# A fused low-rank update on one core: the order of the first loads and stores, and setup work moved between engines

## The chip, the core and the metric

The kernel runs on one core of a Trainium2 chip. The core has a matrix engine (TensorE, PE in the profile), a vector engine (VectorE, DVE), a scalar engine (ScalarE, ACT), a general engine (GpSimd, POOL) and SyncE (SP), which here only issues transfers. Each engine has its own instruction stream; they meet through semaphores. Sixteen DMA engines move data between the chip's memory (HBM) and the on-chip memory (SBUF). The metric is the device time of one execution in microseconds, the median over runs.

## The reference

```python
batch, seq, d_model, r = 16, 512, 768, 16
# x: (16, 512, 768) float32, A: (768, 16), B: (16, 768), scale: 0.5

def reference(x, A, B, scale):
    lora = np.matmul(np.matmul(x, A), B)
    return (x + scale * lora).astype(np.float32)
```

So 25.17 MB are read, a rank-16 product is added to them, and 25.17 MB are written. A and B are 48 KB each.

## The kernel before

**Tiles and parts.** The 8192 rows of `x` are 64 tiles of 128 rows x 768. They are loaded in seven parts, `PARTS = [2, 6, 8, 16, 16, 14, 2]` tiles, one DMA each. Within a part, each of the 128 partitions holds neighbouring rows of memory, so a part of 2 tiles moves in pieces of 6 KB, one of 6 in 18 KB, of 8 in 24 KB, of 16 in 48 KB. All of `x` but the last part has room in SBUF (`x_all`, 62 tiles); the last two tiles go where tiles 0 and 1 were, once these are stored. The 14 tiles of part 5 land last of the others, and until then their room (`spare`) is lent to the setup: `a_rows`, `a_t`, `w_one`, `b_rows`, `b_half`, `pick`.

**Setup.** GpSimd zeroes `a_rows` (L175), `b_rows` (L176), `pick`, `w_bd` and `y_bd`, and makes `pick` a selection pattern. A (L139) and B (L143) are loaded into every eighth row. VectorE transposes A (L214) and makes `w_one` with three small casts (L221); ScalarE copies `w_one` to the four diagonal blocks of `w_bd` (L201). ScalarE casts B to fp16 (`b_half`, L195), TensorE spreads it by `pick` (L290), and ScalarE copies the result to `b_mm` (L198).

**Groups.** The tiles are worked on in eight groups of 8, each in two halves of 4 (`h` = 0, 1):

1. `narrowed` (L171): a half is cast to fp16 in `xh[h]`, half 0 by ScalarE, half 1 by GpSimd. It waits for the loads of its tiles and, by `s_y`, for the matmuls that read the half before.
2. `turned` (L230): VectorE transposes the half in 32x32 blocks.
3. `projected` (L260): TensorE multiplies by `w_bd` in 24 matmuls and leaves x A in `ps_yt`; `s_y` counts the halves.
4. ScalarE (L209) scales that into the diagonal blocks of `y_bd`, four small instructions for a group.
5. `raised` (L277): TensorE multiplies by `b_mm` into `lora_ps`, two tiles at a time, in one of two buffers.
6. `summed` (L235): VectorE adds that to `x_all`, two tiles at a time.

TensorE runs this as a loop of eight passes: the first pass raises an empty group ahead of the first projection, and each pass raises the group before. VectorE's order is written out by hand: the transpose of a half of the next group, then the adds of two pairs of this one. So an engine that waits in its own order holds up all that stands behind it there.

**Transfers.** All of them are issued by SP, in this order: loads of parts 0 and 1, A (once its room is zeroed), B (once its room is zeroed), loads of parts 2, 3 and 4; then, after the first projection (`s_y`), the load of part 5 into the lent room; then the stores of `STORES`, each of which waits on `s_sum` until the groups that it holds are added (a count of groups + 2, raised by TensorE in `raised(1)` of the pass after the one that raises the group), or on `s_last` for the last group. After the store of part 1, SP waits for the store of part 0 to land (`s_out0`) and issues the load of part 6. One queue takes all of it in order.

**The end.** GpSimd waits for the last add, clears most of the semaphores, waits for the stores, and clears the others.

Of the kernel before, what the change touches and what calls it, by code (L numbers as in the profile page):

```python
# [13 lines left out]
PARTS = [2, 6, 8, 16, 16, 14, 2]  # L14
# [6 lines left out]
APART = 8  # L21
# [3 lines left out]
def kernel(  # L25
# [8 lines left out]
    nc = tc.nc  # L34
    fp32 = mybir.dt.float32
    P = 128
    Q = 32
    NQ = P // Q
# [4 lines left out]
    R = A.shape[1]  # L43
    NC = D // 64
# [6 lines left out]
    def sb(name, shape, dtype):  # L51
        return nc.alloc_sbuf_tensor(name, shape, dtype).ap()
# [11 lines left out]
    def lent(n):  # L64
        taken[0] += n
        return spare[:, ds(taken[0] - n, n)]
# [6 lines left out]
    a_t = lent(2 * R * Q).rearrange("p (k r c) -> p k r c", k=2, r=R)  # L73
    w_one = lent(NC * R)[0:Q].bitcast(MM_DT).rearrange("p (c k r) -> p c k r", c=NC, k=2)
    b_rows = lent(D)
    b_half = lent(D // 2).bitcast(MM_DT)
    pick = lent(P // 2).bitcast(MM_DT).rearrange("p (b r) -> p b r", b=NQ)
    w_bd = sb("w_bd", [P, NC, 2, P], MM_DT)
    b_mm = sb("b_mm", [P, D], MM_DT)
    xh = [sb(f"xh{h}", [P, SUB, D], MM_DT) for h in range(2)]  # L80
    y_bd = sb("y_bd", [P, GROUP, P], MM_DT)
    lora = [ps(f"lora_ps{i}", [P, 2, D]) for i in range(2)]
    y_ps = ps("ps_yt", [P, GROUP, Q])

    sems = []

    def sem(name):
        sems.append(nc.alloc_semaphore(name))
        return sems[-1]


    parts = []
# [7 lines left out]
    def memory(t2, i, s, n):  # L100
        S = PARTS[i]
        return t2[ds(parts[i], S * P), :].rearrange("(p s) d -> p s d", s=S)[:, ds(s, n), :]

    def held(i, s, n):
        return tiles(where.index((i, s)), n)

    def tiles(t, n):
        return x_all[:, ds(t % ROOM, n), :]

    s_load = [sem(f"s_load{i}") for i in range(len(PARTS))]  # L110
    s_a, s_b = sem("s_a"), sem("s_b")
    s_ready, s_brows, s_pick, s_zero = sem("s_ready"), sem("s_brows"), sem("s_pick"), sem("s_zero")
    s_w, s_bh, s_bp, s_bm = sem("s_w"), sem("s_bh"), sem("s_bp"), sem("s_bm")
    s_narrow = [sem(f"s_narrow{h}") for h in range(2)]
    s_y, s_spread = sem("s_y"), sem("s_spread")
    s_turned = [sem(f"s_turned{h}") for h in range(2)]
    s_lora = sem("s_lora")

    s_free = [sem(f"s_free{p}") for p in range(PAIRS)]

    s_sum, s_last, s_out0, s_out = sem("s_sum"), sem("s_last"), sem("s_out0"), sem("s_out")

    MMS = 2 * NC
    STORES = [
        (0, 0, 2), (1, 0, 6), (2, 0, 8), (3, 0, 16), (4, 0, 16), (5, 0, 8), (5, 8, 6), (6, 0, 2)
    ]

    section = ExitStack()
# [2 lines left out]
    def on_sync(e):  # L131
        def load(i):
            ld = (i, 0, PARTS[i])
            e.dma_start(out=held(*ld), in_=memory(x2, *ld)).then_inc(s_load[i], 16)

        load(0)
        load(1)
        e.wait_ge(s_ready, 1)
        e.dma_start(  # L139
            out=a_rows[0 : NC * APART : APART, :], in_=A.rearrange("(c e) r -> c (e r)", e=64)  # L140
        ).then_inc(s_a, 16)
        e.wait_ge(s_brows, 1)
        e.dma_start(out=b_rows[0 : R * APART : APART, :], in_=B).then_inc(s_b, 16)  # L143
        for i in range(2, len(PARTS) - 2):
            load(i)

        e.wait_ge(s_y, 1)
        load(len(PARTS) - 2)
        for st in STORES:
            i, s, n = st  # L150
            groups = where.index((i, s + n - 1)) // GROUP + 1
            if groups < NG:

                e.wait_ge(s_sum, groups + 2)
            else:
                e.wait_ge(s_last, 1)
            ins = e.dma_start(out=memory(out2, *st), in_=held(*st))
            ins.then_inc(s_out if i else s_out0, 16)
            if i == 1:
                e.wait_ge(s_out0, 16)  # L160
                load(len(PARTS) - 1)

    def narrowed(e, copy, g, h):
        t = g * GROUP + h * SUB
        for i in dict.fromkeys(where[t + k][0] for k in range(SUB)):
            e.wait_ge(s_load[i], 16)
        if g:
            e.wait_ge(s_y, 2 * g + h - 1)
        n = SUB if (t + SUB - 1) // ROOM == t // ROOM else SUB // 2
        for k in range(0, SUB, n):  # L170
            last = copy(out=xh[h][:, ds(k, n), :], in_=tiles(t + k, n))  # L171
        last.then_inc(s_narrow[h], 1)

    def on_gpsimd(e):
        e.memset(a_rows[0 : NC * APART], 0.0).then_inc(s_ready, 1)  # L175
        e.memset(b_rows, 0.0).then_inc(s_brows, 1)  # L176

        e.sem_inc(s_spread, 1)
        for p, s in enumerate(s_free):
            e.sem_inc(s, 1 if p < 2 else 2)  # L180
        e.memset(pick, 0.0).then_inc(s_pick, 1)
        e.memset(w_bd.rearrange("p c k m -> p (c k m)").bitcast(fp32), 0.0)  # L182
        e.memset(y_bd.rearrange("p s m -> p (s m)").bitcast(fp32), 0.0)  # L183
        e.wait_ge(s_pick, 1)
        e.affine_select(  # L185
            out=pick, in_=pick, compare_op=mybir.AluOpType.not_equal, fill=1.0, base=0,
            pattern=[[0, NQ], [-APART, Q]], channel_multiplier=1,
        ).then_inc(s_zero, 1)
        for g in range(NG):
            narrowed(e, e.tensor_copy, g, 1)  # L190

    def on_scalar(e):
        e.wait_ge(s_zero, 1)
        e.wait_ge(s_b, 16)
        e.copy(out=b_half, in_=b_rows).then_inc(s_bh, 1)  # L195
        narrowed(e, e.copy, 0, 0)
        e.wait_ge(s_bp, 1)
        e.copy(out=b_mm, in_=lora[0][:, 0, :]).then_inc(s_bm, 1)  # L198
        e.wait_ge(s_ready, 3)
        for b in range(NQ):  # L200
            last = e.copy(out=w_bd[ds(b * Q, Q), :, :, ds(b * Q, R)], in_=w_one)  # L201
        last.then_inc(s_w, 1)
        for g in range(NG):
            if g + 1 < NG:
                narrowed(e, e.copy, g + 1, 0)
            e.wait_ge(s_y, 2 * g + 2)
            for b in range(NQ):
                q = ds(b * Q, Q)
                last = e.mul(out=y_bd[q, :, q], in_=y_ps[q, :, :], mul=sc)  # L209
            last.then_inc(s_spread, 1)  # L210

    def on_vector(e):
        e.wait_ge(s_a, 16)
        e.transpose(  # L214
            out=a_t[0 : NC * APART].rearrange("i k r c -> i (k r) c"),
            in_=a_rows[0 : NC * APART].rearrange("c (i k r) -> c (k r) i", k=2, r=R),
        ).then_inc(s_ready, 1)
        e.wait_ge(s_ready, 2)
        EACH = Q // APART
        for b in range(NC // EACH):  # L220
            last = e.tensor_copy(  # L221
                out=w_one[:, ds(b * EACH, EACH), :, :],
                in_=a_t[ds(b * Q, Q)].rearrange("i k r (c n) -> i c k r n", n=APART)[..., 0],
            )
        last.then_inc(s_ready, 1)

        def turned(g, h):
            e.wait_ge(s_narrow[h], g + 1)
            v = xh[h].bitcast(fp32)
            e.transpose(out=v, in_=v).then_inc(s_turned[h], 1)  # L230

        def summed(g, p):
            xs = tiles(g * GROUP + 2 * p, 2)
            e.wait_ge(s_lora, (g + 1) * PAIRS + p + 1)
            ins = e.tensor_tensor(out=xs, in0=xs, in1=lora[p % 2], op=mybir.AluOpType.add)  # L235
            if g + 1 < NG or p + 2 < PAIRS:
                ins.then_inc(s_free[p], 1)
            elif p + 1 == PAIRS:
                ins.then_inc(s_last, 1)

        turned(0, 0)

        e.wait_ge(s_lora, 1)
        turned(0, 1)
        for g in range(NG):
            for h in range(2):
                if g + 1 < NG:
                    turned(g + 1, h)
                summed(g, 2 * h)
                summed(g, 2 * h + 1)  # L250

    def on_tensor(e):
# [15 lines left out]
        def raised(p):  # L268
# [16 lines left out]
                mms[2].then_inc(s_sum, 1)  # L285
            mms[-1].then_inc(s_lora, 1)

        e.wait_ge(s_bh, 1)
        for n0, w in ((0, 512), (512, 256)):
            last = e.matmul(  # L290
                lora[0][:, 0, ds(n0, w)], pick.rearrange("p b r -> p (b r)"),
                b_half[:, ds(n0, w)], start=True, stop=True,
            )
        last.then_inc(s_bp, 1)
        e.wait_ge(s_bm, 1)
        e.wait_ge(s_w, 1)
        with e.Fori(0, NG):
            for h in range(2):
                raised(2 * h)
# [2 lines left out]
        for p in range(PAIRS):  # L302
            raised(p)

    on_sync(nc.sync)
    on_gpsimd(nc.gpsimd)
    on_scalar(nc.scalar)
    on_vector(nc.vector)
    on_tensor(nc.tensor)

    nums = [s.num for s in sems]
    assert nums == list(range(nums[0], nums[0] + len(nums)))

    nc.gpsimd.wait_ge(s_last, 1)
    nc.gpsimd.sem_clear(range(nums[0], s_sum.num))
    nc.gpsimd.wait_ge(s_out, (len(STORES) - 1) * 16)
    nc.gpsimd.sem_clear(range(s_sum.num, s_out.num + 1))
    section.close()


# [33 lines left out]
```

## Time and profile before

| what | value |
|---|---|
| median of 3 runs | 125.58 us (125.11 to 126.81) |
| the profiled execution | 124.85 us |
| its span, first to last instruction | 122.7 us |
| HBM read, written | 25.26 MB, 25.17 MB, 411 GB/s over the span |
| DMA queue | 2216 packets, 96.8% of 16 engines' span |
| PE, PEld, DVE, ACT, POOL busy | 46%, 30%, 68%, 32%, 21% |
| adds (L235), 32 | 54.1 us, 1733 ns each |
| transposes (L230), 16 | 28.2 us, 1765 ns each |
| casts (L171) on POOL, ACT | 22.1 us, 22.0 us; 2.75 us for half a group |
| mean granted TensorE clock | 0.901 |

The span is what the profile shows of the program; the device time holds some 2 us more around it. Busy shares are of the span. "PEclk" is the clock granted to TensorE in tenths of full speed, "PEld" its weight loads. In the tables by stretch each engine has its busy us and number of instructions, then come the clock, the share of the DMA engines in use, and GB/s, where a packet counts in the stretch in which it starts. A row of SP ("SPq") is the issue of a transfer, not the transfer. "issue" in the chain is time in which an engine waited for nothing that the profile shows.

### The profile page before, as it was taken

The numbers are of one execution on the slowest core, as the hardware profiler recorded it, in microseconds if no ns is written. First come the engines' busy times: TensorE is split into PE (matmuls) and PEld (weight loads), VectorE is DVE, ScalarE is ACT, GpSimd is POOL, SyncE is SP. The second block draws the span as 40 slices with busy tenths as digits, with TensorE's granted clock in tenths as the row PEclk, the third lists the DMA queues.
The fourth block names the chain that finished last, engine by engine and source line by source line (L and its number), as shares of the span: only waits on it lengthen the run. The fifth ranks groups of instructions, "written<-read, shape, count | busy, mean of one in ns | idle before, by whom it ended". The sixth has DMA issues, their size and how long they took to land.

```text
span 122.7 us, 1317 instructions
## 1 busy us (share of the span) xinstructions
PE 56.3 (46%) x530; PEld 37.1 (30%) x530; DVE 83.9 (68%) x52; ACT 38.7 (32%) x47; POOL 26.2 (21%) x19
## 2 busy tenths in 40 slices
PE   0000206976755764844845775576497545000000
PEld 0000003855343452533614534345354422000000
DVE  0003751418999999999999999999979979600000
ACT  0002992092193534254084072353400310000000
POOL 7503500026017008006204401700530000000000
PEclk9999999999999999999999999998559999655555
DMA  3999998899799699999599999899796996898994
GB/s 88 439 433 403 449 529 385 385 513 465 305 513 481 288 513 449 449 435 435 202 449 413 479 401 553 353 497 465 321 497 272 513 497 272 385 513 385 415 413 198
DMA packets 2216, 50.43 MB, mean 411 GB/s; under 512 B 268, under 2 KB 268, under 8 KB 808
## 3 DMA queue, kind: packets, MB, share of 16 engines
q1 hardware_dynamic: 2216, 50.43, 96.8%
HBM read 25.26 MB, written 25.17 MB: 411 GB/s over the span
## 4 chain that ended last, share of the span: by engine, by line
DVE 54%; PE 12%; DMA 7%; ACT 6%; issue 5%; POOL 1%; SPq 1%; POOLq 0%; ACTq 0%
DVE x_sb L235 38%; DVE xh L230 16%; DMA x_sb<-in_B_dram 7%; PE ps_yt L260 6%; PE lora_ps L277 6%; ACT xh L171 2%; ACT w_bd L201 2%; ACT y_bd L209 1%; POOL x_sb L175 1%; SPq L139 1%; ACT x_sb L195 1%; ACT b_mm L198 1%; ACT L195 0%; POOLq L349 0%; SPq L129 0%
## 5 line engine op out<-in xcount | busy, mean ns | idle before, releaser
L235 DVE TENSOR_TENSOR x_sb<-x_sb,lora_ps 128x1536 f32<-128x1536 f32 x32 | 54.1, 1733 | 2.3 <-PE lora_ps L277 2.3
L277 PE MATMUL lora_ps<-b_mm,y_bd 128*128 128x512 f16 (+1 forms) x144 | 30.3, 348 | 25.5 <-ACT y_bd L209 10.0
L171 POOL CAST xh<-x_sb 128x3072 f16<-128x3072 f32 (+1 forms) x9 | 22.1, 2465 | 63.1 <-PE ps_yt L260 56.6
L230 DVE STREAM_TRANSPOSE xh<-xh 128x1536 f32<-128x1536 f32 x16 | 28.2, 1765 | 8.7 <-ACT xh L171 5.9
L171 ACT CAST xh<-x_sb 128x3072 f16<-128x3072 f32 x8 | 22.0, 2751 | 27.5 <-PE ps_yt L260 22.7
L260 PE MATMUL ps_yt<-xh,w_bd 128*128 128x128 f16 x384 | 26.4, 226 | 8.2 <-DVE xh L230 8.2
L260 PEld LDWEIGHTS ps_yt<-xh,w_bd 128*128 128x128 f16 x384 | 24.4, 100 | 13.5 <-issue 13.1
L277 PEld LDWEIGHTS lora_ps<-b_mm,y_bd 128*128 128x128 f16 x144 | 12.7, 101 | 39.0 <-issue 21.9
L209 ACT ACTIVATE y_bd<-ps_yt 32x256 f16<-32x256 f32 x32 | 12.0, 375 | 20.8 <-PE ps_yt L260 20.5
L214 DVE STREAM_TRANSPOSE x_sb<-x_sb 96x1024 f32<-96x1024 f32 x1 | 1.9, 1933 | 11.2 <-DMA x_sb<-in_A_dram 11.2
L290 PE MATMUL lora_ps<-x_sb 128*128 128x512 f16 (+1 forms) x2 | 0.8, 514 | 13.7 <-ACT x_sb L195 13.7
L195 ACT ACT_TABLE_LOAD x1 | 1.3, 1283 | 11.6 <-DMA x_sb<-in_B_dram 11.6
L290 PEld LDWEIGHTS lora_ps<-x_sb 128*128 128x128 f16 x2 | 0.1, 108 | 13.7 <-ACT x_sb L195 13.7
L201 ACT COPY w_bd<-x_sb 32x384 f16<-32x384 f16 x4 | 2.0, 508 | 0.0
L221 DVE CAST x_sb<-x_sb 32x128 f16<-32x128 f32 x3 | 1.5, 508 | 0.1
L182 POOL MEMSET w_bd<- 128x1536 f32 x1 | 1.4, 1382 | 0.0
L175 POOL MEMSET x_sb<- 96x1024 f32 x1 | 0.9, 948 | 0.5 <-SPq L129 0.5
L195 ACT CAST x_sb<-x_sb 128x768 f16<-128x768 f32 x1 | 0.8, 832 | 0.0
L198 ACT CAST b_mm<-lora_ps 128x768 f16<-128x768 f32 x1 | 0.8, 799 | 0.0
L176 POOL MEMSET x_sb<- 128x768 f32 x1 | 0.7, 736 | 0.0
L183 POOL MEMSET y_bd<- 128x512 f32 x1 | 0.5, 525 | 0.0
L185 POOL TENSOR_SCALAR_AFFINE_SELECT x_sb<-x_sb 128x128 f16<-128x128 f16 x1 | 0.3, 309 | 0.0
(5 smaller groups left out, 0.6 us busy)
## 6 DMA issues: line engine op xcount, KB each, us to landing
x_sb<-in_x_dram SPq DMA_DIRECT2D x2, 6144.0 KB, 36.2
out_dram<-x_sb SPq DMA_DIRECT2D x2, 6144.0 KB, 19.7
out_dram<-x_sb SPq DMA_DIRECT2D x2, 3072.0 KB, 14.4
x_sb<-in_x_dram SPq DMA_DIRECT2D x1, 5376.0 KB, 37.1
out_dram<-x_sb SPq DMA_DIRECT2D x2, 2304.0 KB, 21.4
x_sb<-in_x_dram SPq DMA_DIRECT2D x1, 3072.0 KB, 15.2
x_sb<-in_x_dram SPq DMA_DIRECT2D x1, 2304.0 KB, 9.9
x_sb<-in_x_dram SPq DMA_DIRECT2D x2, 768.0 KB, 5.9
```

What stands on the lines that cost most here:

```text
L171: last = copy(out=xh[h][:, ds(k, n), :], in_=tiles(t + k, n))
L175: e.memset(a_rows[0 : NC * APART], 0.0).then_inc(s_ready, 1)
L195: e.copy(out=b_half, in_=b_rows).then_inc(s_bh, 1)
L198: e.copy(out=b_mm, in_=lora[0][:, 0, :]).then_inc(s_bm, 1)
L201: last = e.copy(out=w_bd[ds(b * Q, Q), :, :, ds(b * Q, R)], in_=w_one)
L209: last = e.mul(out=y_bd[q, :, q], in_=y_ps[q, :, :], mul=sc)
L214: e.transpose(out=a_t[0 : NC * APART].rearrange("i k r c -> i (k r) c"), in_=a_rows[0 : NC * APART].rearrange("c (i k r) -> c (k r) i", k= ...
L221: last = e.tensor_copy(out=w_one[:, ds(b * EACH, EACH), :, :], in_=a_t[ds(b * Q, Q)].rearrange("i k r (c n) -> i c k r n", n=APART)[..., 0],)
L230: e.transpose(out=v, in_=v).then_inc(s_turned[h], 1)
L235: ins = e.tensor_tensor(out=xs, in0=xs, in1=lora[p % 2], op=mybir.AluOpType.add)
L260: mm = e.matmul(y_ps[:, ds(h * SUB, SUB), :], w_bd[:, c, k, :], xv[:, :, c, :, k], start=(m == 0), stop=(m == MMS - 1),)
L277: mms.append(e.matmul(t[:, k, ds(n0, w)], y_bd[:, 2 * p + k, :], b_mm[:, ds(n0, w)], start=True, stop=True,))
```

## The change

- The store of part 2 (8 tiles, 24 KB pieces) is put ahead of those of parts 0 and 1. All three then wait for the second group.
- SP issues A between the loads of parts 0 and 1. SP also does the first increments of `s_spread` and `s_free`, which GpSimd did; that of `s_free[1]` comes after the first `raised` (`s_lora`).
- B is issued by ScalarE, on its own queue, once its room is zeroed.
- `w_one` and the four copies to `w_bd` are made by GpSimd, each of which waits for the one before; VectorE and ScalarE no longer have them.
- ScalarE copies `b_mm` ahead of its first cast of `x`, and VectorE's transpose of the second half no longer waits for `s_lora`. The wait on `pick` goes from ScalarE to TensorE.
- A wait on a load is left out where the engine has waited for that load before.
- GpSimd no longer clears the semaphores by itself; the clear at the program's end covers all of them.

```diff
     STORES = [
-        (0, 0, 2), (1, 0, 6), (2, 0, 8), (3, 0, 16), (4, 0, 16), (5, 0, 8), (5, 8, 6), (6, 0, 2)
+        (2, 0, 8), (0, 0, 2), (1, 0, 6), (3, 0, 16), (4, 0, 16), (5, 0, 8), (5, 8, 6), (6, 0, 2)
     ]
...
         load(0)
-        load(1)
+
+        e.sem_inc(s_spread, 1)
+        for p, n in ((0, 1), (2, 2), (3, 2)):
+            e.sem_inc(s_free[p], n)
         e.wait_ge(s_ready, 1)
         e.dma_start(
             out=a_rows[0 : NC * APART : APART, :], in_=A.rearrange("(c e) r -> c (e r)", e=64)
         ).then_inc(s_a, 16)
-        e.wait_ge(s_brows, 1)
-        e.dma_start(out=b_rows[0 : R * APART : APART, :], in_=B).then_inc(s_b, 16)
-        for i in range(2, len(PARTS) - 2):
+        for i in range(1, len(PARTS) - 2):
             load(i)
+
+        e.wait_ge(s_lora, 1)
+        e.sem_inc(s_free[1], 1)
...
+    here = set()
+
     def narrowed(e, copy, g, h):
         t = g * GROUP + h * SUB
         for i in dict.fromkeys(where[t + k][0] for k in range(SUB)):
-            e.wait_ge(s_load[i], 16)
+            if (h, i) not in here:
+                here.add((h, i))
+                e.wait_ge(s_load[i], 16)
...
     def on_gpsimd(e):
...
-        e.sem_inc(s_spread, 1)
-        for p, s in enumerate(s_free):
-            e.sem_inc(s, 1 if p < 2 else 2)
...
+        e.wait_ge(s_pick, 2)
+        e.wait_ge(s_ready, 3)
+        EACH = Q // APART
+        for b in range(NC // EACH):
+            e.tensor_copy(
+                out=w_one[:, ds(b * EACH, EACH), :, :],
+                in_=a_t[ds(b * Q, Q)].rearrange("i k r (c n) -> i c k r n", n=APART)[..., 0],
+            ).then_inc(s_w, 1)
+            e.wait_ge(s_w, b + 1)
+        for b in range(NQ):
+            e.tensor_copy(
+                out=w_bd[ds(b * Q, Q), :, :, ds(b * Q, R)], in_=w_one
+            ).then_inc(s_w, 1)
+            e.wait_ge(s_w, NC // EACH + b + 1)
...
     def on_scalar(e):
-        e.wait_ge(s_zero, 1)
+        e.wait_ge(s_brows, 1)
+        e.dma_start(out=b_rows[0 : R * APART : APART, :], in_=B).then_inc(s_b, 16)
         e.wait_ge(s_b, 16)
         e.copy(out=b_half, in_=b_rows).then_inc(s_bh, 1)
-        narrowed(e, e.copy, 0, 0)
         e.wait_ge(s_bp, 1)
         e.copy(out=b_mm, in_=lora[0][:, 0, :]).then_inc(s_bm, 1)
-        e.wait_ge(s_ready, 3)
-        for b in range(NQ):
-            last = e.copy(out=w_bd[ds(b * Q, Q), :, :, ds(b * Q, R)], in_=w_one)
-        last.then_inc(s_w, 1)
+        narrowed(e, e.copy, 0, 0)
...
         turned(0, 0)
-
-        e.wait_ge(s_lora, 1)
         turned(0, 1)
...
+        e.wait_ge(s_pick, 2)
         e.wait_ge(s_bh, 1)
...
-        e.wait_ge(s_w, 1)
+        e.wait_ge(s_w, NC * APART // Q + NQ)
...
-    nc.gpsimd.wait_ge(s_last, 1)
-    nc.gpsimd.sem_clear(range(nums[0], s_sum.num))
+    nc.gpsimd.wait_ge(s_out0, 16)
     nc.gpsimd.wait_ge(s_out, (len(STORES) - 1) * 16)
-    nc.gpsimd.sem_clear(range(s_sum.num, s_out.num + 1))
     section.close()
```

More of the change, by code (lines that the diff above doesn't have):

```diff
@@ L83 @@
     y_ps = ps("ps_yt", [P, GROUP, Q])
-    sems = []
     def sem(name):
-        sems.append(nc.alloc_semaphore(name))
-        return sems[-1]
+        return tc.alloc_semaphore(name)
     parts = []
@@ L111 @@
     s_a, s_b = sem("s_a"), sem("s_b")
-    s_ready, s_brows, s_pick, s_zero = sem("s_ready"), sem("s_brows"), sem("s_pick"), sem("s_zero")
+    s_ready, s_brows, s_pick = sem("s_ready"), sem("s_brows"), sem("s_pick")
     s_w, s_bh, s_bp, s_bm = sem("s_w"), sem("s_bh"), sem("s_bp"), sem("s_bm")
@@ L176, in on_gpsimd @@
         e.memset(b_rows, 0.0).then_inc(s_brows, 1)
-        e.sem_inc(s_spread, 1)
-        for p, s in enumerate(s_free):
-            e.sem_inc(s, 1 if p < 2 else 2)
         e.memset(pick, 0.0).then_inc(s_pick, 1)
         e.memset(w_bd.rearrange("p c k m -> p (c k m)").bitcast(fp32), 0.0)
-        e.memset(y_bd.rearrange("p s m -> p (s m)").bitcast(fp32), 0.0)
+        e.memset(y_bd.rearrange("p s m -> p (s m)").bitcast(fp32), 0.0).then_inc(s_ready, 1)
         e.wait_ge(s_pick, 1)
@@ L187, in on_gpsimd @@
             pattern=[[0, NQ], [-APART, Q]], channel_multiplier=1,
-        ).then_inc(s_zero, 1)
+        ).then_inc(s_pick, 1)
+        e.wait_ge(s_pick, 2)
[12 more added lines that the diff above has]
+            e.wait_ge(s_w, NC // EACH + b + 1)
         for g in range(NG):
@@ L217, in on_vector @@
         ).then_inc(s_ready, 1)
[L218 to L225, printed above, removed]
         def turned(g, h):
@@ L309 @@
     on_tensor(nc.tensor)
-    nums = [s.num for s in sems]
-    assert nums == list(range(nums[0], nums[0] + len(nums)))
-    nc.gpsimd.wait_ge(s_last, 1)
-    nc.gpsimd.sem_clear(range(nums[0], s_sum.num))
+    nc.gpsimd.wait_ge(s_out0, 16)
     nc.gpsimd.wait_ge(s_out, (len(STORES) - 1) * 16)
-    nc.gpsimd.sem_clear(range(s_sum.num, s_out.num + 1))
     section.close()
```

## The prediction

> **What bounds the kernel now.** I read the page first, then stretches of the span, then the chain, the waits and SP's own timeline. The page:
>
> ```profile
> span 122.7 us, 1317 instructions
> PEclk9999999999999999999999999998559999655555
> DMA  3999998899799699999599999899796996898994
> q1 hardware_dynamic: 2216, 50.43, 96.8%
> ```
>
> One queue, SP's, holds the 16 DMA engines 96.8% of the span; the busiest compute engine, VectorE, has 68%. So the end is set by 50.43 MB of traffic, and time can be won only where the engines stand idle: the start, a hole, the end. The stretches (the last two columns are the share of DMA engines in use and GB/s, each row's bytes counted where it starts):
>
> ```profile
> 2.00:3.00 1.00, 0.00 (x0) 0.00 (x0) 0.00 (x0) 0.00 (x0) 1.00 (x3) 1.00 0.88 240
> 5.00:89.50 84.50, 46.73 (x453) 31.52 (x454) 68.77 (x43) 37.16 (x43) 21.55 (x9) 0.97 1.02 432
> 90.20:91.80 1.60, 1.60 (x11) 1.02 (x10) 1.60 (x1) 0.00 (x0) 0.00 (x0) 0.56 0.00 0
> 93.70:121.40 27.70, 5.42 (x44) 2.98 (x44) 11.64 (x7) 1.50 (x4) 0.00 (x0) 0.71 1.00 426
> ```
>
> Nothing moves before 2.0 us; then 5 to 89.5 is full; between 90.2 and 91.8 no row starts. Is that a hole, or only rows that start in step? SP's timeline decides:
>
> ```profile
> 0.97 0.86 SPq L134 DMA_DIRECT2D x_sb<-in_x_dram  x2
> 1.93 0.90 SPq L139 DMA_DIRECT2D x_sb<-in_A_dram  x1
> 2.88 0.55 SPq L143 DMA_DIRECT2D x_sb<-in_B_dram  x1
> 63.60 5.78 SPq L157 DMA_DIRECT2D out_dram<-x_sb  x2
> 91.02 16.85 SPq L157 DMA_DIRECT2D out_dram<-x_sb  x4
> ```
>
> The 63.60 row's second store (part 3) was issued at its end, 69.05; the next (part 4) only at 91.02. Behind it 32 tiles, 12.58 MB, went out from 91.85 to 121.4, 426 GB/s; ahead of it lay 64 loaded and 32 stored tiles, 37.85 MB, at that rate 88.9 us, from 2.0 to some 91.0. New rows came at 91.85. The hole is thus about 0.8 us; with 420 and 429 GB/s, the rates of 30 to 60 and of 2 to 90, 0 to 1.6. I take 0.7.
>
> Why was that store late? It waits for `s_sum`, which follows VectorE's adds. The chain:
>
> ```profile
> 2.88 8.61 DMA x_sb<-in_B_dram
> 29.39 3.42 DVE x_sb L235 x2
> 37.80 1.68 DVE xh L230
> 84.52 2.51 PE ps_yt L260 x24
> 87.03 1.67 issue
> 88.70 1.45 PE lora_ps L277 x4
> ```
>
> Setup hangs on B, which lies behind 2.36 MB of load 1; the first add comes at 29.39; from there VectorE runs without a break, 10.0 us a group (37.80 to 57.75 is two), until 84.5, where TensorE at clock 0.50 stretches a group. From 69.05 to 91.02 is 21.97 for two groups: that cost 2.0 us.
>
> **The change part by part.**
>
> *A between loads 0 and 1.* SP issues load 0 at 0.97; its four new increments lie in the wait for the first memset (ends at 1.90); A takes 1.93 to 2.83; load 1 comes at 2.88 instead of about 1.42. Queued behind A are loads 1 to 4; the first user of them is the engines' queue itself. From issue to first row load 0 took 1.0 us, part 4's store 0.8, so load 1 is ready at 3.7 to 3.9. Load 0's 0.79 MB take 1.83 us plus 0.44 lost in the 240 GB/s ramp: busy until 4.3, with A's 48 KB 4.4. So the cover is 0.5 us. Best 0, worst, if the lag doubles to 2.0 us, 0.5 idle; I take 0.1. A lands by about 4.4 plus the 1.2 that it took before (load 1 and A were through at 10, the transpose began at 11.21), 5.6, not 11.2.
>
> *B on ScalarE's queue.* It waits for the memset's end at 2.58, so ScalarE issues it by 3.2. Landing: at best 4.5 (1.0 us of lag, 0.3 of rows), at worst 11.5 as before, behind load 1. Nearer the first, since its queue holds nothing else. The 1.28 us table load now runs in B's wait instead of after it. Then 0.83, the two matmuls 0.82, `b_mm` 0.80: ready between 7.5 and 14.0.
>
> *`w_one` and `w_bd` to GpSimd.* VectorE gives up 3 x 0.51, ScalarE 4 x 0.51. GpSimd has no such row: its 128x3072 cast takes 2.75 us, 0.86 ns an element plus some 0.1 (its smallest memset), so 0.21 and 0.43, together 2.4; from above the costliest of VectorE's own rows there, 1.0 each, 7.0. With some 0.1 for each of 7 waits on itself, 3.1 to 7.7; I take 4. After A's transpose (5.6 + 1.93 = 7.5) they end between 10.6 and 15.2. Behind them on GpSimd waits its first cast, which needs load 1 at 11.3 anyway.
>
> *First group.* ScalarE casts as load 1 lands, 11.35 to 14.1 (13.60 before); transposes at 14.1 and, the wait on `s_lora` gone, at 15.9; 24 matmuls to 18; the other half's to 20.7 to 22.6; ScalarE's cast of group 1 needs load 2 (3.47 + 15.2 = 18.7) and ends at 21.45; its four 0.38 muls, then matmuls: first add at 24 to 25.5, 4 to 5 us earlier. With the worst B or GpSimd it is 1 to 2 later.
>
> *What is late next.* Not all of this survives. Group 2 lies in load 3:
>
> ```profile
> 33.26 2.75 ACT L171 CAST xh<-x_sb 128x3072 f16<-128x3072 f32 x1 [4.82 <-DMA x_sb<-in_x_dram]
> ```
>
> That load's place in the DMA traffic does not move, so the cast again ends at 36.0, and VectorE's transpose of group 2 comes at 36.05 instead of 37.80. The gain left is 1.75 us. All later adds move by that: store 4 is issued at 89.27, its rows are ready at 90.1, before the queue is dry at 91.0. The hole goes: -0.7.
>
> *Order of stores.* Stores 0 and 1, issued at 39.12, now wait with store 2 until the second group's `s_sum`, 39.12 + 10.0 - 1.75 = 47.4. Behind that wait stand only later stores and load 6; the queue holds loads until 61 (part 5's: issued 24.19, landed 37.1 later), so nobody misses them. Store 0 is through at 61 + 7.4 + 1.8 = 70.2 instead of 62.8; load 6, which waits for it, is issued at 70.6 instead of 63.22, with store 1's 5.5 us still queued, and lands at 78. GpSimd casts its tiles at 87.19, less 1.75, so 7 us of cover are left. If it were gone, each us there would delay the last two tiles, whose store has another 7 us of queue ahead of it. Bytes and rows are the same: 0.
>
> *Shorter programs and semaphores.* Repeated waits on loads already seen are left out, in which the engines did not wait: 0. GpSimd's last clear leaves the tail; the final one clears 37 semaphores, not 6. Neither is on the page; between the last packets at 121.4 and the end at 122.7 there are 1.3 us in all, so -0.3 to +0.3; I take +0.1.
>
> *Sum.* Against the profiled execution's own 124.85 (span 122.7, 2.15 around it): -0.7 + 0.1 + 0 + 0.1 = -0.5, 124.35, span 122.2. The shown median, 125.58, lies 0.73 above that execution; the same step gives 125.1. From the bounds: hole 0 to -1.6, start 0 to 0.5, tail -0.3 to 0.3: 123.7 to 126.4. A measurement of this kernel tells about 2% from no change, 2.5 us; no term here is that large.
>
> **The gate, by row and by rule.**
>
> ```profile
> 84.80:91.60 6.80, 5.13 (x34) 3.51 (x32) 5.99 (x4) 1.50 (x4) 2.88 (x2) 0.50 0.80 347
> ```
>
> TensorE was busy 5.13 of these 6.80 us and yet ran at 0.50. From 78.0 to 84.8 it was busy 4.68 us, and no wait of it inside the groups is over 1.7. So a closing can come again, earlier or later. [...]
>
> **Rivals.**
>
> *N, nothing comes of it.* GpSimd's copies or B take so long that group 2 gains nothing and the hole stays, or other executions have no hole to lose. For it: a single execution shows the hole. Against: 1.75 us come even with the worst of either. 125.58 + 0.2 = 125.8. Chance 0.15.
>
> *S, the start (slower than before).* Load 1's rows come after load 0's are through, because A's 0.90 us issue is on its way and B is issued beside it. It decides once rows are later than 4.4, and then shifts the whole queue one for one. With a lag of 2.0 us and B's 0.55 us issue on top, 1.0 idle instead of 0.1: 126.0. Against: 0.5 us of cover. Chance 0.10.
>
> *G, the gate closes more often ahead of part 4's store.* 2.0 us each. One more than now puts its issue at 91.3, its rows at 92.1, hole 1.0 after all: 126.1; a third, 128.1. Chance 0.10, of it 0.04 for the third or worse.
>
> *F, the fetch behind the span is shortened.* Past the last instruction, from 122 on, the instructions' own queue moves two packets:
>
> ```profile
> DMA packets 2, 0.02 MB, mean 2 GB/s; under 512 B 0, under 2 KB 0, under 8 KB 0
> q14 instruction: 2, 0.02, 0.7%
> ```
>
> They start some 1.0 us apart, within the 2.15 us around the span. As built, ScalarE's program goes from 68 to 61 instructions, VectorE's from 65 to 61, GpSimd's from 53 to 54. If each packet belongs to one of these two, one saved gives 124.1, all 2.15 gone 122.9. Against: TensorE's, the longest, stays. Chance 0.13. [...]
>
> **How the numbers follow.** Forecast 0.52, N 0.15, F 0.13, S 0.10, G 0.10. The likeliest gives 125.1. To leave out no more than 2 in 10 the range reaches down into F and up to S and G: 123.7 to 126.7. Faster by over 2% (under 123.1) is F's far end, 0.04; slower by over 2% (over 128.1) needs a third closing, or S and G together, 0.04; the rest 0.92.
>
> **What would show it.** Right: A's transpose near 5.6, `b_mm` before 9, first add near 24 to 25, the wait on load 3 before 33.3 longer than now with group 2's transpose near 36.0, part 4's store issued near 89, rows starting throughout 90 to 92, load 6 landed before 80, span near 122.2. Wrong: a stretch without rows near 4 us (S), a clock of 0.50 in two stretches before 89 (G), the group 2 transpose still at 37.8 (N), fewer instruction packets behind the span (F).

## The result, and the profile after

The median of the changed kernel is 126.75 us (126.13 to 127.44, 13 runs), that of the kernel before 125.11 (124.90 to 126.81, 13 runs). The ratio is 1.0125, 95% interval 1.0095 to 1.0155: 1.6 us slower, under the 2% line but clear of noise. The profiled execution took 127.44 us, 2.59 more than the one before, with 1.74 us around its span instead of 2.15. It is the longest of the 13, so its rows show the loss at its largest.

The page after. The compute rows hardly moved; the DMA row has lost its full last slices.

```profile
span 125.7 us, 1313 instructions
DMA  2999999899999989999898999998997999899970
q1 hardware_dynamic: 2184, 50.38, 95.0%
q10 hardware_dynamic: 32, 0.05, 0.2%
x_sb<-in_x_dram SPq DMA_DIRECT2D x1, 2304.0 KB, 10.9
```

q10 is ScalarE's queue with B. The last line is load 1: issued at 2.85, it landed 10.9 later, at 13.75. In the kernel before, the same line has 9.9, from 1.42, so 11.3. The issues of the changed kernel:

```profile
0.96 0.38 SPq L130 DMA_DIRECT2D x_sb<-in_x_dram  x1
1.92 0.88 SPq L138 DMA_DIRECT2D x_sb<-in_A_dram  x1
2.60 0.58 ACTq L208 DMA_DIRECT2D x_sb<-in_B_dram  x1
2.85 18.79 SPq L130 DMA_DIRECT2D x_sb<-in_x_dram  x5
91.12 0.33 SPq L157 DMA_DIRECT2D out_dram<-x_sb  x1
```

Who notices: the first cast of group 0 (load 1), the first add, and the cast of group 2 (load 3).

```profile
13.85 2.75 ACT L175 CAST xh<-x_sb 128x3072 f16<-128x3072 f32 x1 [2.23 <-DMA x_sb<-in_x_dram]
27.98 3.42 DVE L238 TENSOR_TENSOR x_sb<-x_sb,lora_ps 128x1536 f32<-128x1536 f32 x2 [2.05 <-PE lora_ps L278]
35.59 2.75 ACT L175 CAST xh<-x_sb 128x3072 f16<-128x3072 f32 x1 [8.55 <-DMA x_sb<-in_x_dram]
```

Load 3 was issued in the same place of the queue, at 3.96 instead of 4.09, and yet its user starts at 35.59 instead of 33.26. The 2.3 us that load 1 was late are still there 22 us later. The stretches at the start and the end, first of the kernel before, then of the changed one:

```profile
4.00:8.00 4.00, 0.00 (x0) 0.00 (x0) 0.00 (x0) 0.00 (x0) 0.82 (x3) 1.00 1.06 441
120.00:121.00 1.00, 0.00 (x0) 0.00 (x0) 0.00 (x0) 0.00 (x0) 0.00 (x0) 0.50 1.03 424
121.00:122.00 1.00, 0.00 (x0) 0.00 (x0) 0.00 (x0) 0.00 (x0) 0.00 (x0) 0.50 0.11 43
```

```profile
4.00:8.00 4.00, 0.00 (x0) 0.00 (x0) 1.90 (x1) 0.50 (x1) 1.19 (x4) 1.00 1.05 358
90.20:91.80 1.60, 1.28 (x12) 0.67 (x10) 1.60 (x2) 0.00 (x0) 0.99 (x1) 1.00 0.57 246
120.00:121.00 1.00, 0.00 (x0) 0.00 (x0) 0.00 (x0) 0.00 (x0) 0.00 (x0) 0.50 1.01 424
121.00:122.00 1.00, 0.00 (x0) 0.00 (x0) 0.00 (x0) 0.00 (x0) 0.00 (x0) 0.50 0.46 191
122.00:123.00 1.00, 0.00 (x0) 0.00 (x0) 0.00 (x0) 0.00 (x0) 0.00 (x0) 0.50 0.21 86
123.00:124.50 1.50, 0.00 (x0) 0.00 (x0) 0.00 (x0) 0.00 (x0) 0.00 (x0) 0.50 0.06 25
```

Three readings. From 4 to 8 us the share of engines in use is the same, 1.05 against 1.06, but GB/s falls from 441 to 358: the engines were not idle, their rows took longer. The hole at 90.2 to 91.8 is mostly filled. And the end is no longer common to all engines: at full rate, 430 GB/s in all, one of 16 moves 27, so the 86 GB/s of 122 to 123 are, by estimate, some three engines that still work while the others are done. The trace also has the single arrivals that raise a transfer's semaphore, 16 for each load and store of `x`; they are read here as one from each of the 16 engines, though the trace does not name the engine. Load 1's are spread over 2.75 us (11.02 to 13.77; before, 10.12 to 11.27), those of loads 2, 3 and 4 over 2.70, 2.70 and 2.69, those of the store of part 4 over 2.91 (106.90 to 109.81; before, 106.78 to 107.12), and the last of all comes at 124.39 instead of 121.76.

### The profile page after: what moved, and what is told of

It reads as the page before. It is cut to its first block, busy times and chain, and to the rows that moved or that the text cites. A ratio compares the mean times of both kernels' runs of the same rounds, so it can differ in the third digit from the quotient of the medians.

```text
span 125.7 us, 1313 instructions
## 1 busy us (share of the span) xinstructions
PE 58.2 (46%) x530; PEld 38.3 (30%) x530; DVE 82.3 (66%) x49; ACT 36.9 (29%) x43; POOL 29.3 (23%) x26
## 4 chain that ended last, share of the span: by engine, by line
DVE 49%; DMA 25%; ACT 5%; PE 3%; SPq 2%; POOL 1%; issue 1%; POOLq 0%
DVE x_sb L238 34%; DMA x_sb<-in_x_dram 25%; DVE xh L233 15%; ACT y_bd L220 2%; ACT xh L175 2%; PE lora_ps L278 2%; PE ps_yt L261 1%; SPq L130 1%; POOL x_sb L179 1%; SPq L138 1%; POOLq L346 0%; SPq L125 0%
## 5 line engine op out<-in xcount | busy, mean ns | idle before, releaser
L278 PE MATMUL lora_ps<-b_mm,y_bd 128*128 128x512 f16 (+1 forms) x144 | 31.4, 359 | 25.1 <-ACT y_bd L220 15.3
L233 DVE STREAM_TRANSPOSE xh<-xh 128x1536 f32<-128x1536 f32 x16 | 28.1, 1764 | 15.2 <-ACT xh L175 15.2
L261 PE MATMUL ps_yt<-xh,w_bd 128*128 128x128 f16 x384 | 27.1, 230 | 11.6 <-DVE xh L233 11.6
L261 PEld LDWEIGHTS ps_yt<-xh,w_bd 128*128 128x128 f16 x384 | 25.0, 102 | 17.4 <-issue 17.1
L278 PEld LDWEIGHTS lora_ps<-b_mm,y_bd 128*128 128x128 f16 x144 | 13.2, 104 | 38.9 <-issue 22.3
L199 POOL COPY w_bd<-x_sb 32x384 f16<-32x384 f16 x4 | 2.0, 500 | 0.2
L193 POOL CAST x_sb<-x_sb 32x128 f16<-32x128 f32 x3 | 1.1, 382 | 2.9 <-DVE x_sb L225 2.8
## 6 DMA issues: line engine op xcount, KB each, us to landing
out_dram<-x_sb SPq DMA_DIRECT2D x2, 3072.0 KB, 17.7
x_sb<-in_x_dram SPq DMA_DIRECT2D x1, 3072.0 KB, 17.7
x_sb<-in_x_dram SPq DMA_DIRECT2D x1, 2304.0 KB, 10.9
```

Source lines behind the costliest of these rows:

```text
L199: e.tensor_copy(out=w_bd[ds(b * Q, Q), :, :, ds(b * Q, R)], in_=w_one).then_inc(s_w, 1)
L261: mm = e.matmul(y_ps[:, ds(h * SUB, SUB), :], w_bd[:, c, k, :], xv[:, :, c, :, k], start=(m == 0), stop=(m == MMS - 1),)
L278: mms.append(e.matmul(t[:, k, ds(n0, w)], y_bd[:, 2 * p + k, :], b_mm[:, ds(n0, w)], start=True, stop=True,))
```

## The experiments

T1 is the theory that these lines suggest: load 1 was issued too late for its rows to run at full pace, a few engines lost more than the others, and the end waits for the slowest, if each engine moves its own fixed share of every transfer (the author's assumption; no run names the engine of a row). The table sets the runs side by side (load 1's landing is its issue plus the time to landing; group 2's cast is the first user of load 3); the ratio is to executions of the kernel before that were measured alongside, whose median was 125.11 to 125.24; it is formed from the single times and not from the two medians.

| kernel | load 1 issued | landed | group 2's cast | median | ratio (95%) |
|---|---|---|---|---|---|
| before | 1.42 | 11.3 | 33.26 | 125.11 | |
| changed | 2.85 | 13.8 | 35.59 | 126.75 | 1.0125 (1.0095 to 1.0155) |
| e1 load 1 before A | 1.41 | 11.4 | 33.27 | 125.00 | 0.995 (0.991 to 0.999) |
| e2 B by SP | 2.86 | 13.7 | 35.66 | 126.73 | 1.0098 (1.0062 to 1.0134) |
| e3 both back | 1.41 | 11.2 | 33.12 | 125.15 | 0.9959 (0.9921 to 0.9997) |
| e4 stores back | 2.85 | 13.6 | 35.42 | 126.74 | 1.010 (1.0063 to 1.0138) |
| e5 A and B by ScalarE | 1.38 | 11.4 | 33.26 | 125.05 | 0.9979 (0.9945 to 1.0014) |
| e6 load 1 alone late | 2.75 | 13.8 | 35.81 | 126.76 | 1.0104 (1.0045 to 1.0163) |
| e7 load 1 at 1.92 | 1.92 | 12.8 | 35.06 | 125.80 | 1.0028 (0.9983 to 1.0074) |
| e8 two clears | 1.41 | 11.3 | 33.27 | 124.85 | 0.9965 (0.9936 to 0.9994) |
| e9 long programs | 1.41 | 11.6 | 33.41 | 125.24 | 0.9983 (0.995 to 1.0017) |
| e10 longer load 0 | 2.85 | 11.7 | 33.56 | 125.47 | 1.0004 (0.9969 to 1.0038) |
| e11 e1 with two clears | 1.41 | 11.3 | 33.16 | 124.71 | 0.9946 (0.9916 to 0.9977) |
| e12 loads spaced | 2.85 | 13.1 | 34.88 | 126.56 | 1.0084 (1.0044 to 1.0124) |

### Which part costs: e1, e2, e3, e4

**e1**, the changed kernel with

```diff
         load(0)
+        load(1)
...
-        for i in range(1, len(PARTS) - 2):
+        for i in range(2, len(PARTS) - 2):
             load(i)
```

> The changed kernel with load 1 issued again right behind load 0, A behind it; B stays on ScalarE's queue. [...] Then load 1's last landing is back from 13.8 to about 11.3, the last packet near 121, and the time 1.5 to 2.5 us under the changed kernel's 126.75: 124.2 to 125.2. Theory T2 (second queue: B's rows on ScalarE's queue stall single engines amid load 1): load 1's last landing stays over 12.5 and the time is 126 to 127. Theory T3 (order of stores): no change, 126.7.

125.00 us, and load 1 lands at 11.4. One line moved, and the whole loss is gone: as T1 has it (11.3, and 124.2 to 125.2), T2 and T3 not. (The engines had not run dry in the changed kernel: load 1's first rows begin at 4.45 us, load 0's last ends at 5.08.)

**e2**, the changed kernel with B on SP's queue behind load 1:

```diff
-        for i in range(1, len(PARTS) - 2):
+        load(1)
+        e.wait_ge(s_brows, 1)
+        e.dma_start(out=b_rows[0 : R * APART : APART, :], in_=B).then_inc(s_b, 16)
+        for i in range(2, len(PARTS) - 2):
             load(i)
...
     def on_scalar(e):
-        e.wait_ge(s_brows, 1)
-        e.dma_start(out=b_rows[0 : R * APART : APART, :], in_=B).then_inc(s_b, 16)
         e.wait_ge(s_b, 16)
```

> The changed kernel with B issued by SP behind load 1, one queue for all; A stays between loads 0 and 1. T1: load 1 still comes at 2.85, so the time stays at 126 to 127 and load 1's last landing over 12.5. T2: without the second queue no engine lags, load 1's last landing is at or under 12.2 and the time 124.5 to 125.5. T3: 126.7. B is back behind load 1, so b_mm is later than in the changed kernel, which alone should cost nothing (group 2 still waits for load 3).

126.73 us, load 1 at 13.7. The second queue is not the cause; T2 falls.

**e3**, both of these edits, so that SP issues load 0, load 1, A and B as before:

> The changed kernel with the issue order of before: load 0, load 1, A, B, all by SP; setup on GpSimd, store order, left-out waits and the single clear stay as changed. T1 and T2: load 1 lands as before at 11.3 with a spread near 1.2 us between the engines, and the time is 124.2 to 125.2. T3: 126.5 or more. If it is under the kernel before (125.1), what is left of the change is a gain.

125.15 us. What is left of the change is no loss. The interval of the ratio lies just under 1, but the medians are equal within 0.1 us (125.24 for the kernel before, measured alongside); where the difference comes from is told below, under the hole.

**e4**, the changed kernel with the stores in the old order:

```diff
-        (2, 0, 8), (0, 0, 2), (1, 0, 6), (3, 0, 16), (4, 0, 16), (5, 0, 8), (5, 8, 6), (6, 0, 2)
+        (0, 0, 2), (1, 0, 6), (2, 0, 8), (3, 0, 16), (4, 0, 16), (5, 0, 8), (5, 8, 6), (6, 0, 2)
```

> The changed kernel with the stores in the order of before (2, 6, 8 tiles). T1 and T2: bytes and rows are the same and the queue holds loads until 61 us in either order, so 126.4 to 127.1, the lag of single engines still there. T3 (the stores' order costs): 125.3 or less.

126.74 us: the order of the stores is worth nothing either way; T3 falls. By chance this execution issued part 4's store at 92.15, and rows were scarce around it (90 to 92: 197 GB/s). Yet its last packet ended at 124.00, the changed kernel's at 124.05. That is a first sign on what a hole is worth.

### Lateness alone, and how much: e6, e7, e5, e10

**e6** is e3 with one more wait, and nothing between the two loads:

```diff
         load(0)
+        e.wait_ge(s_pick, 1)
         load(1)
```

> The kernel with the issue order of before (load 0, load 1, A, B; 125.15 us), in which SP waits for one more memset ahead of load 1, so that it is issued near 2.8 us, as in the changed kernel, with nothing between it and load 0. T1: the lateness alone brings the lag back: load 1's last landing over 12.5, the 16 engines over 2 us apart, time 126.2 to 127. T1b: no lag, last landing under 12, time 125.1 to 125.8.

126.76 us. The issues, and the stretch after them:

```profile
0.96 2.13 SPq L130 DMA_DIRECT2D x_sb<-in_x_dram  x2
3.40 0.89 SPq L140 DMA_DIRECT2D x_sb<-in_A_dram  x1
```

```profile
4.00:8.00 4.00, 0.00 (x0) 0.00 (x0) 0.00 (x0) 0.00 (x0) 0.81 (x3) 1.00 1.01 349
```

Load 1 starts to be issued at 2.75 (the second of the pair that ends at 3.09), and the 349 GB/s are those of the changed kernel. In the trace load 1's rows begin at 4.2 to 5.4, right behind load 0's, but the first ones take up to 1.8 us instead of 0.7 to 0.9 (e3). So lateness is enough, without A between; T1 as expected, T1b not.

**e7** asks how late is too late: e3 with `e.wait_ge(s_ready, 1)` in that place, half a us of lateness instead of 1.3.

> The kernel with the issue order of before (125.15 us; load 1 issued at 1.41), in which SP waits for the first memset ahead of load 1, so that load 1 comes at 1.93 with A behind it: half a us late instead of 1.4. T1 with a threshold (rows must be issued some 2 us ahead of the end of load 0's rows at 4.3): 2.4 us ahead is enough, load 1 lands near 11.4, time 125.0 to 125.4. T1 in proportion (each us of lateness costs): 0.5/1.4 of the 1.6 us, load 1 lands near 12.1, time 125.6 to 125.9.

125.80 us, load 1 at 12.8, group 2's cast at 35.06. No threshold at 2.4 us ahead: half a us late already made the slowest engine 1.5 us late. The time falls into the band of the proportional reading; the landing lies above it. The landing is what shows the loss here: the times run from 125.22 to 127.19, and the interval of the ratio takes in 1. From 4 to 8 us the engines moved only 301 GB/s, less than in the changed kernel, but the loss fell more evenly: load 1's arrivals are 1.90 us apart.

**e5** has A early without a late load 1: load 1 behind load 0, A and B by ScalarE.

```diff
         load(0)
+        load(1)
...
-        e.wait_ge(s_ready, 1)
-        e.dma_start(
-            out=a_rows[0 : NC * APART : APART, :], in_=A.rearrange("(c e) r -> c (e r)", e=64)
-        ).then_inc(s_a, 16)
-        for i in range(1, len(PARTS) - 2):
+        for i in range(2, len(PARTS) - 2):
             load(i)
...
     def on_scalar(e):
+        e.wait_ge(s_ready, 1)
+        e.dma_start(
+            out=a_rows[0 : NC * APART : APART, :], in_=A.rearrange("(c e) r -> c (e r)", e=64)
+        ).then_inc(s_a, 16)
         e.wait_ge(s_brows, 1)
```

> The changed kernel with load 1 right behind load 0 on SP's queue and both A and B issued by ScalarE: A early without a late load 1. T1 (the late issue of load 1): load 1 is on time, so its last landing is near 11.4 and the time 124.7 to 125.3, as with load 1 ahead of A (125.0); A still lands by 6. Rival T1b (it is A's rows, or any small transfer that comes between the rows of loads 0 and 1 on single engines): load 1's last landing is over 12.5 and the time 126 or more.

125.05 us, as T1 has it. A came at 8.7, not by 6, as load 1's rows, issued at 1.38, were there first. The earlier setup moved the first add to 24.5 us, the earliest of all runs, and did not shorten this execution: group 2 still starts at 33.26, when load 3 lands.

**e10** keeps A between the loads and load 1's issue at 2.85, but gives it more cover:

```diff
-PARTS = [2, 6, 8, 16, 16, 14, 2]
+PARTS = [4, 4, 8, 16, 16, 14, 2]
...
-        (2, 0, 8), (0, 0, 2), (1, 0, 6), (3, 0, 16), (4, 0, 16), (5, 0, 8), (5, 8, 6), (6, 0, 2)
+        (2, 0, 8), (0, 0, 4), (1, 0, 4), (3, 0, 16), (4, 0, 16), (5, 0, 8), (5, 8, 6), (6, 0, 2)
```

> The changed kernel (126.75 us) with parts of 4 and 4 tiles at the start instead of 2 and 6 (the stores of these two likewise). A stays between loads 0 and 1 and load 1 is issued at 2.85, but load 0's rows now last to some 6.2 us. T1 (what counts is how far ahead of the end of load 0's rows load 1 is issued): 3.3 us ahead, no lag of single engines, load 1's last landing near 11.5, time 124.7 to 125.4. Rival T1c (what counts is the time itself, as when A, B and four loads are issued in the same 2 us): the lag stays, 126.2 to 127.

125.47 us; load 1's last landing is 11.7, and load 3's user is nearly back:

```profile
33.56 2.75 ACT L175 CAST xh<-x_sb 128x3072 f16<-128x3072 f32 x1 [9.67 <-DMA x_sb<-in_x_dram]
```

Same issue time, most of the loss gone, so the time of the issue alone does not decide. The runs fit the reading that it is how far ahead of the end of the rows in progress a transfer is issued. Counted to the prediction's estimate of that end, 4.3 us (6.2 in e10), 2.9 us (before, e1) is enough, 3.3 (e10) nearly so for a longer load 0, 2.4 (e7) is not, 1.5 (changed, e2, e6) costs it all. This is argued and not shown, since e10 also changes the sizes of both loads. And what went in e10 is the unevenness: the mean of load 1's 16 arrivals is 11.29, against 11.56 in the changed kernel and 10.60 before, but their spread is 0.91.

**e12** asks whether load 1's rows are held up by the issue of the loads behind it:

```diff
-        for i in range(1, len(PARTS) - 2):
+        load(1)
+        e.wait_ge(s_a, 16)
+        for i in range(2, len(PARTS) - 2):
             load(i)
```

> The changed kernel (126.75 us) in which SP, after load 1, waits for A's landing (5.5 us) before it issues loads 2 to 4; these then come at 5.6 to 7, still 4 us ahead of the end of load 1's rows. Rival T1c (the issue of the following loads, 3.35 to 4.9, takes from what load 1's rows need): the first rows of load 1 take 0.7 to 0.9 us again instead of 0.8 to 1.9, last landing under 12, time 125 to 125.6. T1 (only load 1's own lateness counts): first rows as long as before this edit, last landing 13 or more, time 126.2 to 127.2.

126.56 us, load 1 at 13.1, its first rows still up to 1.75 us. Load 1's own lateness is enough, and T1c falls; the issue of the loads behind it has at most a small part, as load 1 landed at 13.6 to 13.8 in the other runs with such an issue (changed, e2, e4, e6). Why a row that is issued late also runs slowly no run here shows.

### The end of the program: e8, e9, e11

**e8** is e3 with GpSimd's two clears of before:

```diff
-    nc.gpsimd.wait_ge(s_out0, 16)
+    nc.gpsimd.wait_ge(s_last, 1)
+    nc.gpsimd.sem_clear(range(nums[0], s_sum.num))
     nc.gpsimd.wait_ge(s_out, (len(STORES) - 1) * 16)
+    nc.gpsimd.sem_clear(range(s_sum.num, s_out.num + 1))
```

The list of semaphore numbers that these lines use, `nums`, comes back with them.

> The kernel with the issue order of before (125.15 us, span 123.2), with GpSimd's two clears of before in place of the single one at the end. If the single clear of 37 semaphores costs what the traces show (0.24 us against 0.07, and a branch with a wait), the stretch from the last landing to the end is 0.92 us again instead of 1.26, and the time 124.7 to 124.9. If that stretch hides behind something else, 125.15.

124.85 us. From the last landing to the end it is 0.91 us in the trace, 1.27 in e3: the single clear cost its third of a us.

**e9** is e3 with waits that are already fulfilled at the end of two programs, two to an instruction, so 8 and 5 more instructions (68 and 66 as built):

```diff
             last.then_inc(s_spread, 1)
+        for _ in range(16):
+            e.wait_ge(s_b, 16)
...
                 summed(g, 2 * h + 1)
+        for _ in range(10):
+            e.wait_ge(s_a, 16)
```

> The kernel with the issue order of before (125.15 us), with 8 waits that are long fulfilled added to the end of ScalarE's program and 5 to VectorE's, so that these have 68 and 66 instructions again (61 and 61 without). If the programs' length sets the instruction fetches behind the span, two of them are back and the time outside the span is 2.15 us instead of 1.8, the median some 0.35 higher: 125.4 to 125.6. If not, 1.8 and 125.15.

125.24 us. Behind the span the packets are back, where e3 and the changed kernel have none:

```profile
q14 instruction: 2, 0.02, 0.5%
```

But the profiled execution has 1.97 us around its span with them (125.47 and 123.5) and e3 the same 1.97 without (125.17 and 123.2). So in these runs the programs' length decides whether these fetches come, and they cost no time that these runs show (125.24 against 125.15).

**e11** joins what was left: load 1 first, B by ScalarE (e1), and the two clears (e8).

> A version meant to beat both: load 1 right behind load 0, A behind it on SP, B on ScalarE's queue (125.0 us with the single clear), and GpSimd's two clears of before, which took 0.36 us off the end. Sum: 125.0 - 0.3 = 124.7, ratio to before 0.993 to 0.996. If the clear's gain does not add, 125.0.

124.71 us, 0.9946 (0.9916 to 0.9977): 0.5 us under the kernel before (125.19, measured alongside) and 2.0 under the changed one. The transfers are not done earlier than before: the last arrival is at 121.99, before at 121.76, and the span is 122.9 against 122.7. What is shorter is the time around the span, 1.8 against 2.15, and no run here shows why.

## Why the prediction was wrong

**A between the loads: the term that failed.** The prediction gave load 1 a cover of 0.5 us, because its rows would be ready at 3.7 to 3.9 and load 0's would last to 4.4 (in the changed kernel the last of them ended at 5.08). The rows did follow load 0's closely, and no gap opened in which all engines stood still. The step was wrong in two ways. It took it that a row that is ready in time runs at full pace; the 358 GB/s from 4 to 8 us are 83 under before, 0.33 MB, or some 0.8 us of all engines. And it took the 16 engines for one queue. The loss fell unevenly, 2.5 us on the slowest of them, and it is the slowest that ends the kernel. The term was +0.1 and measured +2.6 in the profiled execution, the longest of its kernel (last landing 124.39 against 121.76), and +1.6 in the medians (changed against e3). Rival S had the right sign and place and the right start, load 1's issue behind A's, at 0.9 and 10%, but with an idle gap where the runs show slow rows. Its "decides once rows are later than 4.4" is refuted by e6, where the first rows began at 4.2 and the loss was whole.

That the loss stays with the same engines is how the trace of the changed kernel reads. The arrivals of loads 2, 3 and 4 keep the spread of load 1 (2.70, 2.70 and 2.69 us against 2.75), and the last four of the 16 stand at nearly the same distances each time (0.45, 1.21 and 0.54 us in load 1; 0.40, 1.20 or 1.21 and 0.54 in the other three), as a fixed share of each engine would leave them; which engine an arrival comes from no run shows. In step with that, load 1 lands 2.5 us later than before, load 2 2.35 (3.35 + 17.7 against 3.47 + 15.2), load 3's user starts 2.3 later, and the last store lands 2.6 later.

Not all of a lag need reach the end, though. Against e3, load 4 is 2.5 us late in the changed kernel, 2.7 in e6, 2.5 in e2, 1.8 in e12 and 1.9 in e7, nearly as load 1 was; the last store is late by 2.5, 1.6, 1.1, 1.3 and 0.4. Where the rest is made up after load 4 is left open. It fits that the medians lost less than the profiled execution of the changed kernel.

**The hole: a second term that failed, unnoticed in the total.** It was to give -0.7. In the changed kernel part 4's store was issued at 91.12 and not near 89, since load 3 was late. In e1 and e3 it was issued at 89.75 and 89.84, close to the 89.27 foreseen, and they have no hole (e3 moved 430 GB/s in the stretch of the first line):

```profile
90.20:91.80 1.60, 1.54 (x24) 1.40 (x25) 1.60 (x2) 0.00 (x0) 0.00 (x0) 1.00 0.87 369
120.00:121.00 1.00, 0.00 (x0) 0.00 (x0) 0.00 (x0) 0.00 (x0) 0.00 (x0) 0.50 0.46 191
121.00:122.00 1.00, 0.00 (x0) 0.00 (x0) 0.00 (x0) 0.00 (x0) 0.00 (x0) 0.50 0.03 12
```

These are e1's. Most engines are done half a us earlier than before (191 against 424 GB/s from 120 to 121), yet the last store lands at 121.94, before at 121.76. In the kernel before, the hole let the slow engines catch up: the arrivals of the store of part 3 are spread over 1.2 us (91.16 to 92.36), those of the store of part 4 over 0.34 (106.78 to 107.12). Only the engines ahead waited in it, and their waiting was free. From the last arrival of part 3's store to the last of all it is 29.40 us with the hole (92.36 to 121.76) and 29.38 without it (e1, 92.56 to 121.94). The 0.7 was the mean of all engines; the slowest engine's own wait was near nothing.

That holds for the traced execution of 124.85 us. Of 112 executions of the kernel before, 26 took 126.0 us or more; of the 70 with load 1 on time and the earlier setup (e1, e3, e5, e8, e9, e11), none took more than 125.72. So what is left of the change may well rid the kernel of its long executions, and e3's ratio lies under 1 with equal medians because they count in it. None of them was traced, and their cause is open.

**The chain of the first groups.** A's transpose began at 5.58 (5.6 expected), GpSimd's copies took 7.61 to 11.13, 3.5 us (4 expected), group 0 no longer waited for the setup. B landed at 8.99, so that `b_mm` was ready at 11.62, within 7.5 to 14.0 but not before 9. But the first add came at 27.98 instead of 24 to 25.5, and group 2 at 38.37 instead of 36.05, since loads 1, 2 and 3 were late. e5 shows the sequence as it was foreseen, 24.5 and 36.04, and that its median is no better for it (125.05 against 125.13). "That load's place in the DMA traffic does not move" was the sentence that failed: load 3 did not move in the queue, but its last arrival did (35.56 against 33.24 us).

**Order of stores.** 0 expected, 0 found (e4). Load 6 landed at 80.8, not before 80, with 7.5 us left to its cast (88.31).

**The end.** +0.1 expected, +0.34 found, just outside its bounds of 0.3 either way (e8). **Around the span** -0.4, expected 0. Rival F named what went, the two fetches, and priced one at 1.0 us, but e9 shows that they are not what the time hangs on (125.24 us with them, 125.15 without in e3). Why the two packets come and go between 61 and 68 instructions no run shows. The rest differs from kernel to kernel (1.74 to 1.97 in the changed ones, 2.15 before) and is left open.

**The gate.** It closed (the granted clock fell to 0.50) once ahead of part 4's store, at 37.9 to 44.7. The first four matmuls of `raised` in it took 1.45 us, at full clock 0.82 (at 31.45), and VectorE's pairs of adds then began 5.10 and 4.99 us apart (41.48, 46.58, 51.57). There TensorE had waited 5.2 us for ScalarE, whose order has the cast of load 3's group ahead of the scaling. In the kernel before it closed at 84.8 with no wait of TensorE over 1.7 us in the 10 us ahead of it, so what closes it no run here shows. Rival G's condition, two closings ahead of 89, came about in e1 and e3 (from 37.33 and 64.63, from 36.73 and 74.27), and part 4's store was still issued by 89.84; its price of 2.0 us each did not show in the time.

So 125.1 is the time of the change without A between the loads (e3, 125.15), but by luck and not for the reason given. The hole went there and won nothing, and the base of the sum, 125.58, was a median of three; over 13 executions the kernel before has 125.11.

## What to carry to other kernels

Count DMA engines singly: here the last of a transfer's 16 arrivals set the end (124.39 us in the changed kernel, the first of the last store's at 121.64), a loss on a few of them at the start could stay to the end (0.4 to 2.5 us of 1.8 to 2.7), and the stretch without rows cost next to nothing (29.40 us to the last arrival with it, 29.38 without). Keep the first big transfers back to back and well ahead of the rows in progress (here 2.9 us ahead of their estimated end was enough, 2.4 and 1.5 were not), and let small ones with waits go behind them or on another queue. A setup that ends earlier moves little where the next group waits for its load anyway (in e5 the first add came at 24.5 us and group 2's cast still at 33.26).

## What the runs showed of the hardware that was not expected

- A transfer issued 1.5 us ahead of the estimated end of the rows in progress had no gap before it, but its first rows took up to 1.9 us (changed; 1.8 in e6 and e12) instead of 0.7 to 0.9, and unevenly over the engines: landings 2.2 to 3.1 us apart instead of 1.05 to 1.15.
- A short run-dry of the queue levels the engines: the spread of a store's landings went from 1.2 to 0.34 us across the hole of the kernel before, and from 2.69 to 0.85 in e6, where rows ran short from 91 to 93 (98 GB/s), while e1 and e3, without a hole, end with a spread of 1.3 us.
- ScalarE's program at 60 or 61 instructions and VectorE's at 61 had no instruction fetch behind the span (changed, e3), 68 and 65 or 66 had two (before, e9); the time did not change with them (125.24 us in e9, 125.15 in e3).
